# A column mean over 8192 rows: six row groups loaded in pairs instead of one by one, and no early load of group 60

## The chip, the cores and the metric

The kernel runs on one core of one Trainium2 chip. The metric is the device time of one execution in microseconds, as a median over runs. The engines are named as the profile names them: PE is TensorE (matrix multiplication), DVE is VectorE, ACT is ScalarE, POOL is GpSimd and SP is SyncE, which here issues nearly all DMA transfers.

## The reference

The kernel must compute the mean of each column of a float32 matrix of 8192 x 8192, 268 MB:

```
x = np.random.randn(8192, 8192).astype(np.float32)
np.mean(x, axis=0)
```

Every input element is read once and added once; the output is 8192 numbers. No part of the input is used twice.

## The kernel before, in words

The rows are cut into 64 groups of 128 (group g is the rows 128 g to 128 g + 127), and a group has one row on each of the 128 partitions, 8192 columns, 4096 KB. The columns are counted in sixteen blocks of 512. On chip there are six row buffers of that size: slots 0 to 3 receive loads, `both` (slot 4) holds the sum of a pair, and `acc` (slot 5) is the accumulator.

All loads are issued by SyncE in the order of the program, by the helper `load` (L75); a load waits, where its buffer was used before, for the add that read the buffer last. Two groups can come as one load (`load_rows`, L89): partition p then gets two neighbouring rows, 64 KB in one piece. Which row of a group of rows lands on which partition does not matter, since everything is summed in the end.

- L111 to L116: half a megabyte of group 60 (blocks 14 and 15) goes ahead into a buffer of its own, `early`; then the groups 0 to 3 as one load and 4 and 5 as another, and five blocks of group 63 (9 to 13), also into `early`. VectorE makes three adds of them that leave the sum in `acc`.
- L119 to L133, the main loop: two groups per load, slots 0 and 1 or 2 and 3 in turn. VectorE adds the two rows into `both` and then `both` into `acc`. It runs from group 6 to group 55. At groups 24 and 32, GpSimd adds the pieces in `early` into `acc`, in two parts.
- L135 to L138: groups 56 to 59 come one by one, and each is added straight into `acc`, one add per group.
- L139 to L144: group 60 comes without its last two blocks and VectorE adds fourteen blocks; group 61 comes whole and VectorE adds only the blocks 7 to 15. Blocks 0 to 6 of group 61 are left to TensorE.
- L145 to L152: group 62 comes whole. GpSimd adds its blocks 14, 15 and 8 into `acc` ("the joins" below, L148). Group 63 comes in four pieces (blocks 4 to 7, 0 to 3, 14 and 15, 8); its blocks 9 to 13 were loaded early.

TensorE makes the sums over the partitions, with a 128 x 32 matrix of 1/8192 as the weights, and can add several sources into one result: the accumulator, what is left of groups 61 and 62, and the pieces of group 63. Four column strips of TensorE work side by side: block i goes to strip i modulo 4, and the blocks 8 to 15 are spread over the strips in quarters (`spread`). The list `sums` (L167 to L181) gives the order, and TensorE keeps it: a matmul that waits holds back all behind it. At the end ScalarE and VectorE copy the results out of PSUM, and five small stores write the output; the last one (L219) writes block 8, whose sum over the last piece of group 63 comes last.

The order within each engine is the program's. An add that needs both a landing and the add before it gets the two waits by way of a no-op on ScalarE or GpSimd (L97 to L104), for which VectorE then waits.

Of the kernel before, what the change touches and what calls it, by code (L numbers as in the profile page):

```python
# [9 lines left out]
def kernel(  # L10
# [2 lines left out]
    x: bass.AP,  # L13
    out: bass.AP,
):

    nc = tc.nc
    f32 = mybir.dt.float32
    M, N = x.shape  # L40
    P = nc.NUM_PARTITIONS
    F = 512
    W = F // 4
    G = M // P
# [3 lines left out]
    sb = ctx.enter_context(tc.tile_pool(name="sb", bufs=1))  # L48
    psp = ctx.enter_context(tc.tile_pool(name="psum", bufs=1, space=bass.MemoryType.PSUM))

    bufs = sb.tile([P, U, N], f32, name="bufs")
    both = bufs[:, U - 2, :]
    acc = bufs[:, U - 1, :]
    ones = sb.tile([P, 32], f32, name="ones")
    early = sb.tile([P, 7 * F], f32, name="early")
    tail = sb.tile([P, W], f32, name="tail")
    warm = sb.tile([P, 32], f32, name="warm")
    nc.gpsimd.memset(ones[:], 1.0 / M)  # L58
# [16 lines left out]
    def load(dst, src):  # L75
        ins = tc.keep_in_program_order(nc.sync.dma_start(out=dst, in_=src)).ins  # L76
        k = len(loads)
        over = loads[k - 8:k - 6] if k >= 8 and k % 2 == 0 else []
        tc.declare_no_dep(ins, group="loads", keep=over, reason="the reader of the buffer waited")
        for o in over:  # L80
            tc.add_manual_dep(ins, o.name, sync, reason="covers the next load too")
        tc.add_to_no_dep_group("loads", ins)
        loads.append(ins)
        return ins

    def rows(g, n=1):
        return x[g * P:(g + n) * P, :]

    def load_rows(g, u, n):  # L89
        return load(bufs[:, u:u + n, :], rows(g, n).rearrange("(p j) c -> p j c", j=n))  # L90
# [3 lines left out]
    def add(dst, a, b, dmas):  # L94

        ins = nc.vector.tensor_add(out=dst, in0=a, in1=b).ins  # L96
        if dmas and adds:  # L97
            waiter = nc.scalar if len(adds) % 8 > 1 else nc.gpsimd
            nop = joins[waiter] = tc.keep_in_program_order(waiter.nop()).ins  # L99
            for o in dmas + adds[-1:]:  # L100
                tc.add_manual_dep(nop, o.name, sync, reason="the no-op waits")
            for group in ("loads", "adds"):
                tc.declare_no_dep(ins, group=group, reason="the no-op waited")
            tc.add_manual_dep(ins, nop.name, sync, reason="waits for both at once")  # L104
        elif adds:
            tc.declare_no_dep(ins, group="loads", reason="the add ahead waited")
        tc.declare_no_dep(ins, group="early", reason="the no-op waited, or the add behind it")
        tc.add_to_no_dep_group("adds", ins)
        adds.append(ins)

    load(early[:, 5 * F:], rows(G - 4)[:, 14 * F:])  # L111
    first, second = load_rows(0, 0, 4), load_rows(4, 4, 2)
    load(early[:, :5 * F], rows(G - 1)[:, 9 * F:14 * F])
    add(bufs[:, 2:4, :], bufs[:, 2:4, :], bufs[:, 0:2, :], [first])
    add(bufs[:, 4:6, :], bufs[:, 4:6, :], bufs[:, 2:4, :], [second])
    add(acc, acc, both, [])  # L116
    tc.keep_in_program_order(nc.scalar.copy(out=warm[:], in_=ones[:]))  # L117
    ahead = []
    g = 6  # L119
    while g < G - 8:  # L120
        u = (g + 2) % 4
        dma = load_rows(g, u, 2)
        add(both, bufs[:, u, :], bufs[:, u + 1, :], [dma])
        add(acc, acc, both, ahead)
        ahead = []
        if g in (24, 32):
            lo, hi = (0, 4) if g == 24 else (4, 7)
            cols = slice((9 + lo) * F, (9 + hi) * F)
            ins = tc.keep_in_program_order(nc.gpsimd.tensor_add(  # L129
                out=acc[:, cols], in0=acc[:, cols], in1=early[:, lo * F:hi * F])).ins  # L130
            tc.add_to_no_dep_group("early", ins)
            ahead = [ins]
        g += 2  # L133

    while g < G - 4:  # L135
        row = bufs[:, (g + 2) % 4, :]
        add(acc, acc, row, [load(row, rows(g))])
        g += 1  # L138
    for lo, hi, loaded in [(0, 14, 14), (7, 16, 16)]:  # L139
        row = bufs[:, (g + 2) % 4, :]  # L140
        dma = load(row[:, :loaded * F], rows(g)[:, :loaded * F])
        cols = slice(lo * F, hi * F)
        add(acc[:, cols], acc[:, cols], row[:, cols], [dma])
        g += 1  # L144
    r61, r62, r63 = [bufs[:, (g + 1 + j) % 4, :] for j in range(3)]  # L145
    load(r62, rows(g))
    for cols in [slice(14 * F, 16 * F), slice(8 * F, 9 * F)]:
        joined = tc.keep_in_program_order(nc.gpsimd.tensor_add(  # L148
# [7 lines left out]
    def blocks(row, lo, hi):  # L156
        for i in range(lo, hi):
            sums.append((banks[i // 4], i % 4, 0, row[:, i * F:(i + 1) * F]))
# [5 lines left out]
                at = lo * F + q * n + c  # L164
                sums.append((dst, q, c, row[:, at:at + min(F, n - c)]))

    blocks(acc, 2, 5)  # L167
    blocks(acc, 0, 2)
    blocks(r61, 0, 7)
    blocks(acc, 5, 8)  # L170
    blocks(r62, 0, 8)
    spread(wide, acc, 9, 14, slice(1))
    blocks(r63, 4, 8)
# [83 lines left out]
```

## Time and profile before

| what | us |
|---|---|
| median of three runs (628.39 to 628.57) | 628.53 |
| span of the profiled execution, first to last instruction | 626.4 |
| difference of the two | 2.1 |
| VectorE busy | 529.3 |
| TensorE busy | 13.3 |
| GpSimd busy | 12.0 |
| ScalarE busy | 3.7 |

The profile is of one execution, and its own time is given as its span; what lies around it is taken from the difference in the table. The page has a line of busy slices for each engine: the span is cut into 40, and a digit is the busy share in tenths. A group's line names source line, engine, operation, output and inputs with their sizes, and the count, then total busy time and the mean duration of one in ns, then the idle time ahead and what ended it. In the timeline a line has start, duration, engine, line and operation, the count of merged instructions, and in brackets the idle time before and its releaser. A releaser such as "ACTq L99" is the no-op of the helper, which in turn had waited for a landing. In the chain of waits a line has start, duration and what the time went to.

### The profile page before, as it was taken

The page shows a single profiled execution, that of the slowest core. Times are in us where ns is not written, and L with a number is a line of the kernel's source. Part 1 is how long each engine was busy: PE and PEld are TensorE (multiplying, and loading weights), DVE is VectorE, ACT ScalarE, POOL GpSimd, SP SyncE. Part 2 cuts the span into 40 slices and gives each one's busy share as a digit, 9 for nine tenths or more (in the row PEclk, how much of TensorE's full clock was granted, in tenths as well). Part 3 has the DMA queues.
Part 4 walks back from the last instruction along what each step waited for, and adds up shares of the span by engine and source line. Part 5 has one row for each costly group of instructions (what it writes and reads, how often), then busy time and mean ns, then how long its engine had stood idle before and what let it go on. Part 6 is the DMA issues. An engine that isn't in the chain of part 4 may idle for free.

```text
span 626.4 us, 484 instructions
## 1 busy us (share of the span) xinstructions
PE 13.3 (2%) x126; PEld 4.0 (1%) x126; DVE 529.3 (85%) x60; ACT 3.7 (1%) x6; POOL 12.0 (2%) x10
## 2 busy tenths in 40 slices
PE   0000000000000000000000000000000000000008
PEld 0000000000000000000000000000000000000002
DVE  0028999998888998889998899888898888999992
ACT  0000000000000000000000000000000000000001
POOL 0000000000000000020000200000000000000002
PEclk9999999999999999999999999999999999999999
DMA  8999999999999999999999999999999999999997
GB/s 372 465 402 428 459 410 460 402 469 402 469 402 469 402 469 402 469 402 469 402 465 406 439 431 427 444 410 460 402 469 402 469 402 469 402 435 435 419 435 305
DMA packets 5930, 268.50 MB, mean 429 GB/s; under 512 B 660, under 2 KB 668, under 8 KB 1064
## 3 DMA queue, kind: packets, MB, share of 16 engines
q1 hardware_dynamic: 5912, 268.46, 99.3%
q8 instruction: 1, 0.02, 0.0%
q10 hardware_dynamic: 16, 0.01, 0.0%
q14 instruction: 1, 0.01, 0.0%
HBM read 268.44 MB, written 0.03 MB: 429 GB/s over the span
## 4 chain that ended last, share of the span: by engine, by line
DMA 59%; DVE 30%; another core or an unknown queue 10%; issue 0%; SPq 0%; ACTq 0%; PE 0%; POOL 0%; POOLq 0%
DMA bufs<-in_x_dram 59%; DVE bufs L96 30%; SPq L76 0%; ACTq L99 0%; PE last L183 0%; DVE tail L214 0%; POOL ready L61 0%; POOL ones L58 0%; POOLq L99 0%; POOLq L241 0%
## 5 line engine op out<-in xcount | busy, mean ns | idle before, releaser
L96 DVE TENSOR_TENSOR bufs<-bufs 128x8192 f32<-128x8192 f32 (+3 forms) x59 | 529.0, 8966 | 85.9 <-DMA bufs<-in_x_dram 43.0
L183 PE MATMUL bank<-bufs,ones 128*32 128x512 f32 x62 | 10.0, 716 | 610.3 <-DVE bufs L96 610.0
L129 POOL TENSOR_TENSOR bufs<-bufs,early 128x2048 f32<-128x2048 f32 (+1 forms) x2 | 7.9, 3954 | 348.5 <-DVE bufs L96 348.5
L148 POOL TENSOR_TENSOR bufs<-bufs 128x1024 f32<-128x1024 f32 (+1 forms) x2 | 3.6, 1824 | 258.9 <-DMA bufs<-in_x_dram 258.9
L214 DVE COPY tail<-last 128x128 f32<-128x128 f32 x1 | 0.3, 291 | 8.8 <-PE last L183 8.8
L183 PEld LDWEIGHTS bank<-bufs,ones 128*32 128x32 f32 x62 | 2.2, 121 | 616.4 <-issue 614.5
L198 ACT COPY bufs<-bank 128x512 f32<-128x512 f32 x2 | 1.2, 586 | 617.9 <-PE bank L183 617.9
L183 PE MATMUL wide<-bufs,ones 128*32 128x512 f32 (+1 forms) x32 | 2.5, 432 | 0.0
L117 ACT ACT_TABLE_LOAD x1 | 1.3, 1283 | 0.7 <-PEq L241 0.7
L183 PE MATMUL two<-bufs,ones 128*32 128x256 f32 x16 | 1.2, 380 | 0.0
L183 PEld LDWEIGHTS wide<-bufs,ones 128*32 128x32 f32 x32 | 1.0, 110 | 1.8 <-issue 1.8
L183 PE MATMUL last<-bufs,ones 128*32 128x128 f32 x16 | 0.8, 279 | 0.1
L198 ACT COPY bufs<-wide 128x640 f32<-128x640 f32 x1 | 0.7, 692 | 1.1 <-PE wide L183 1.1
L183 PEld LDWEIGHTS last<-bufs,ones 128*32 128x32 f32 x16 | 0.4, 109 | 1.2 <-issue 0.6
L183 PEld LDWEIGHTS two<-bufs,ones 128*32 128x32 f32 x16 | 0.4, 109 | 0.1
L198 ACT COPY bufs<-two 128x256 f32<-128x256 f32 x1 | 0.4, 372 | 0.1
L117 ACT COPY warm<-ones 128x32 f32<-128x32 f32 x1 | 0.2, 217 | 0.0
L61 POOL TENSOR_TENSOR ready<-ones 128x1 f32<-128x1 f32 x1 | 0.2, 193 | 0.1
L58 POOL MEMSET ones<- 128x32 f32 x1 | 0.1, 125 | 0.3 <-POOLq L241 0.3
L241 POOL MEMSET const-float32-0.0<- 128x1 f32 x1 | 0.1, 98 | 0.2 <-issue 0.2
L241 POOL MEMSET const-bfloat16-1.0<- 128x1 bf16 x1 | 0.1, 102 | 0.0
L241 POOL MEMSET const-uint8-127<- 128x1 uint8 x1 | 0.1, 102 | 0.0
(1 smaller groups left out, 0.1 us busy)
## 6 DMA issues: line engine op xcount, KB each, us to landing
bufs<-in_x_dram SPq DMA_DIRECT2D x6, 4096.0 KB, 20.4
bufs<-in_x_dram SPq DMA_DIRECT2D x1, 3584.0 KB
bufs<-in_x_dram SPq DMA_DIRECT2D x2, 1024.0 KB, 18.7
early<-in_x_dram SPq DMA_DIRECT2D x1, 1280.0 KB
early<-in_x_dram SPq DMA_DIRECT2D x1, 512.0 KB
bufs<-in_x_dram SPq DMA_DIRECT2D x1, 512.0 KB, 19.4
bufs<-in_x_dram SPq DMA_DIRECT2D x27, 29.9
bufs<-in_x_dram SPq DMA_DIRECT2D x1, 256.0 KB, 19.7
```

What stands on the lines that cost most here:

```text
L58: nc.gpsimd.memset(ones[:], 1.0 / M)
L61: nc.gpsimd.tensor_add(out=ready[:], in0=ones[:, 0:1], in1=ones[:, 1:2]))
L96: ins = nc.vector.tensor_add(out=dst, in0=a, in1=b).ins
L117: tc.keep_in_program_order(nc.scalar.copy(out=warm[:], in_=ones[:]))
L129: ins = tc.keep_in_program_order(nc.gpsimd.tensor_add(out=acc[:, cols], in0=acc[:, cols], in1=early[:, lo * F:hi * F])).ins
L148: joined = tc.keep_in_program_order(nc.gpsimd.tensor_add(out=acc[:, cols], in0=acc[:, cols], in1=r62[:, cols])).ins
L183: summed = tc.keep_in_program_order(nc.tensor.matmul(out=dst[32 * q:32 * q + 32, c:c + cols.shape[1]], lhsT=ones[:], rhs=cols, start=all(( ...
L198: return tc.keep_in_program_order(nc.scalar.copy(out=dst, in_=src)).ins
L214: ended = nc.vector.tensor_copy(out=tail[:], in_=last[:]).ins
L241: nc = _bacc.Bacc("TRN2", target_bir_lowering=False, num_devices=1)
```

## The change

Groups 56 to 61 come as three loads of two groups, where they were six loads of one. Groups 56 to 59 are now part of the main loop: both rows into `both`, then into `acc`. Group 60 comes whole beside group 61, so nothing of it is loaded early, and `early` holds only the five blocks of group 63; GpSimd adds them in parts of three and two blocks (they were four and three, with the two blocks of group 60 at the end). VectorE adds all sixteen blocks of group 60 and then the blocks 7 to 15 of group 61; both adds follow the same landing. TensorE's list begins with the seven blocks of group 61, then the blocks 0 to 7 of the accumulator, which before stood around them. What follows in the list is the same.

```diff
-    early = sb.tile([P, 7 * F], f32, name="early")
+    early = sb.tile([P, 5 * F], f32, name="early")
...
-    load(early[:, 5 * F:], rows(G - 4)[:, 14 * F:])
     first, second = load_rows(0, 0, 4), load_rows(4, 4, 2)
-    load(early[:, :5 * F], rows(G - 1)[:, 9 * F:14 * F])
+    load(early[:], rows(G - 1)[:, 9 * F:14 * F])
...
-    while g < G - 8:
+    while g < G - 4:
...
-            lo, hi = (0, 4) if g == 24 else (4, 7)
+            lo, hi = (0, 3) if g == 24 else (3, 5)
...
-    while g < G - 4:
-        row = bufs[:, (g + 2) % 4, :]
-        add(acc, acc, row, [load(row, rows(g))])
-        g += 1
-    for lo, hi, loaded in [(0, 14, 14), (7, 16, 16)]:
-        row = bufs[:, (g + 2) % 4, :]
-        dma = load(row[:, :loaded * F], rows(g)[:, :loaded * F])
-        cols = slice(lo * F, hi * F)
-        add(acc[:, cols], acc[:, cols], row[:, cols], [dma])
-        g += 1
-    r61, r62, r63 = [bufs[:, (g + 1 + j) % 4, :] for j in range(3)]
+    u = (g + 2) % 4
+    dma = load_rows(g, u, 2)
+    add(acc, acc, bufs[:, u, :], [dma])
+    r61 = bufs[:, u + 1, :]
+    add(acc[:, 7 * F:], acc[:, 7 * F:], r61[:, 7 * F:], [])
+    g += 2
+    r62, r63 = [bufs[:, (g + 2 + j) % 4, :] for j in range(2)]
     load(r62, rows(g))
...
-    blocks(acc, 2, 5)
-    blocks(acc, 0, 2)
     blocks(r61, 0, 7)
-    blocks(acc, 5, 8)
+    blocks(acc, 0, 8)
     blocks(r62, 0, 8)
```

## The prediction

> **What bounds the kernel now.** I read the page's busy slices first, then the timeline of the last 120 us, then the chain of waits, and last the windows around the final matmuls.
>
> The page: the DMA engines are full from end to end, VectorE is busy 85%, TensorE only in the last slice.
>
> ```profile
> span 626.4 us, 484 instructions
> ...
> PE   0000000000000000000000000000000000000008
> ...
> DVE  0028999998888998889998899888898888999992
> ...
> DMA  8999999999999999999999999999999999999997
> ```
>
> VectorE's timeline: a pair of groups costs 17.42 us and starts every 19.35 us (510.81, 530.16, 549.50), each time after 1.93 us of idling for the landing. So the stream of loads sets the pace. From 549.50, where the single groups begin to arrive, VectorE runs without a gap, 65.39 us and eight adds.
>
> ```profile
> 510.81 17.42 DVE L96 TENSOR_TENSOR bufs<-bufs 128x8192 f32<-128x8192 f32 x2 [1.94 <-ACTq L99]
> 530.16 17.42 DVE L96 TENSOR_TENSOR bufs<-bufs 128x8192 f32<-128x8192 f32 x2 [1.93 <-POOLq L99]
> 549.50 65.39 DVE L96 TENSOR_TENSOR bufs<-bufs 128x8192 f32<-128x8192 f32 x8 [1.93 <-ACTq L99]
> ```
>
> The same timeline at the end: group 62 lands at 616.28 (TensorE's wait is ended by DMA), after VectorE has finished at 614.9. From 616.28 TensorE works through the remaining sums almost without a gap, and meets the last landing at 623.2.
>
> ```profile
> 616.28 1.92 PE L183 MATMUL bank<-bufs,ones 128*32 128x512 f32 x16 [0.28 <-DMA bufs<-in_x_dram]
> 616.49 3.61 POOL L148 TENSOR_TENSOR bufs<-bufs 128x1024 f32<-128x1024 f32 x2 [258.93 <-DMA bufs<-in_x_dram]
> ...
> 623.23 0.43 PE L183 MATMUL last<-bufs,ones 128*32 128x128 f32 x8
> 623.73 0.29 DVE L214 COPY tail<-last 128x128 f32<-128x128 f32 x1 [8.83 <-PE last L183]
> 624.04 0.50 SPq L201 DMA_DIRECT2D out_dram<-tail  x1
> ```
>
> The chain of waits names the last landing as what the end follows:
>
> ```profile
> 603.45 19.74 DMA bufs<-in_x_dram
> 623.19 0.04 issue
> 623.23 0.47 PE last L183 x8
> ```
>
> So two things end together: the stream (623.19) and TensorE's own work on groups 62 and 63, which had only some 0.26 us of slack (the 256-column sums of group 63 start their second pass at 622.76 and need 0.21 us, so the last sums could have started near 622.97). Anything that delays TensorE's start on group 62 shows at the end almost whole.
>
> **The change, part by part.**
>
> *The loads.* Bytes are the same, only order and size change. Without the early half megabyte of group 60 the first load starts earlier. Its share of the stream: 19.35 us carry 8192 KB, so 512 KB is 1.2 us. Bounds: 0, if the start-up of the first load hides it, and 1.65 us, from the first packet of the early load (1.78 us) to the first large packet (3.4 us) in the DMA records. I take 1.2, the price at the stream's own rate. All later pairs land 1.2 earlier: pair 54 at 549.44 - 1.2 = 548.24, and then pairs 56, 58 and 60 every 19.35: 567.6, 586.9, **606.3**. In before group 61 alone landed at about 616.23 - 9.7 = 606.5, so the stream is worth 0.2 us. Three issues fewer on SyncE (0.33 us each) lie beside transfers that are already queued.
>
> *Issue times.* Group 62's load now waits for the first add of pair 58, which ends at 586.9 + 0.06 + 8.70 = 595.7; the stream is busy with pair 60 until 606.3, a cover of 10.6 us. The four pieces of group 63 go behind it without a VectorE wait, near 597 instead of 602.1. Cost 0.
>
> *GpSimd's early adds* shrink by a block each (from 4.49 and 3.42 us; the 1024-column row is 2.37). VectorE's add beside them is longer (11.21 and 10.12 instead of 8.70 in the chain), but it waits 1.93 us per pair for the stream anyway, and the next load is queued ten microseconds ahead: 0. Without that cover it would be at most 2.5 us once.
>
> *VectorE's last adds*, the term that matters. Single groups let VectorE take 56 to 60 one by one, and only nine blocks of 61 (4.96 us) were left behind group 60. As pairs, 56/57 and 58/59 are worked in their 19.35 us again (17.42 us, idle 1.9 before the next). Then pair 60 lands at 606.3, with all its work still to do:
>
> ```profile
> L96 DVE TENSOR_TENSOR bufs<-bufs 128x8192 f32<-128x8192 f32 x55 | 482.0, 8763 | 40.5 <-ACTq L99 30.6 <-POOLq L99 8.2
> ...
> L96 DVE TENSOR_TENSOR bufs<-bufs 128x4608 f32<-128x4608 f32 x1 | 5.0, 4957 | 0.1
> ```
>
> 606.3 + 0.06 (landing to add, as 549.44 to 549.50) + 8.70 (group 60, undisturbed) + 0.02 + 4.96 (nine blocks) = **620.04**, against 614.9 before: 5.1 us later, and 3.8 us past the time at which group 62 was taken up. The no-op for group 60 stands in GpSimd's queue, ahead of the two joins, which need the same add: nothing else waits there.
>
> *TensorE.* Seven blocks of group 61 run from 606.3, blocks 0 to 6 of the accumulator from 615.1, and block 7 needs the last add, so it starts at 620.09. Behind it, in order, stand all sums over group 62. Block 7 writes the fourth column strip, which block 3 of group 62 needs too; a block's two passes take 0.87 us (eight blocks on four strips from 616.28 to 618.02). So that strip takes up group 62 at 620.09 + 0.87 = 620.96 where it was 616.28: +4.68. The wait for the last landing (0.26) is gone, as group 63 lands by about 623. Sum at the end: **+4.4 us**. Block 7's round is the unknown: 0 if the strips fill the gap, 0.87 if its strip stays last. I take 0.87, since that strip has the same number of pieces as the others.
>
> *GpSimd's joins* (2.37 + 1.28 us) move from 616.5 to about 620.2 and end at 623.9. The 256-column sums need the first at 620.96 + 4.75 = 625.7, the 128-column ones at about 627: 3 us of slack, cost 0. *Stores and copies* keep their distances behind TensorE, so the 2.7 us from the last matmul to the end of the span remain.
>
> *TensorE's rate.* This is the second unknown. The same sixteen matmul instructions took twice as long right after idling as later:
>
> ```profile
> 609.98:613.41 3.43, 3.43 (x16) 0.77 (x17) 0.00 (x0) 1.00 1.07 459
> ...
> 616.28:618.02 1.74, 1.74 (x16) 0.41 (x16) 0.00 (x0) 1.00 1.03 428
> ```
>
> (Windows of the bank sums: stretch, its length, TensorE busy, weight loads, ScalarE, granted clock, DMA share, GB/s.) The granted-clock column says 1.00 in both, so the slow stretch is read from the durations. In before those slow 3.43 us lay ahead of group 62's landing, and the 0.4 us pause before it did not bring them back. Now there are three bursts: 606.3 to about 609.8, 615.1 to 616.9 or 618.5, and the last from 620.1, with pauses of 5.3 and of 1.6 to 3.2 us. If the last burst runs full speed, the extra cost is 0. If it starts slow, 3.43 us of it do half their work: +1.7; the worst I give it is a second stretch of the same, +3.4. I take 0, since the second burst comes between and, if it runs slow, is as long as the stretch after which the rate doubled in before.
>
> [...]
>
> **Sum.** +4.68 - 0.26 = +4.4 on a span of 626.4: 630.8. The median shown (628.53) is 2.1 us above that span; I keep this distance. **632.9 us**, 0.7% slower. A measurement of this kernel tells about 0.2% (1.3 us) from no change.
>
> **The rivals.**
>
> *TensorE starts its last burst slow.* For it: the 3.43 us row, and two new pauses. Against: a pause of 0.4 us did nothing, and the second burst warms it. It gives 632.9 + 1.7 = 634.6, between 633.4 and 636.3.
>
> *The adds stay beside the transfers* (the other side). If the stream delivered pair 60 early enough that VectorE ended before 616.28 - 0.87 + 0.26 = 615.7, the last landing would set the end again, at about 628.3. That needs pair 60 at 602.0 instead of 606.3: three pairs in 53.8 us, 17.9 each. Against it: 23 pairs from 104.37 to 549.44 took 19.35 each, and the stream's 432 GB/s is the same in that stretch and in the stretch of the single groups.
>
> *The early load is worth more and block 7's round is hidden*: -0.45 and -0.87 give 631.6, about 631.0 to 632.1.
>
> **How the numbers follow.** Forecast 0.66 (its own range 632.1 to 633.4), slow burst 0.28, smaller delay 0.04, adds hidden 0.02. The range 632.1 to 635.0 leaves out the last two (0.06) and the upper part of the slow burst (about 0.1). Slower holds all but the hidden case: 0.98; that case is split into 0.01 and 0.01. The early load's lower bound of 0 would give 634.1 and lies inside.
>
> **What would show it.** In the changed kernel: VectorE's adds in pairs of 17.42 us every 19.35 us up to pair 58, then one run of 8.70 + 4.96 us from about 606.3 to 620.0; TensorE idle until then, and its wait before the last burst ended by VectorE instead of DMA; GpSimd's joins released by VectorE; no wait for a landing in the chain's last 14 us. I am wrong if pair 60 lands elsewhere than 605.8 to 607.5, if the last burst is not about 8 us long (longer: slow clock), or if TensorE takes up group 62 before VectorE is done.

## The result and the profile after

The changed kernel takes 633.84 us in the median of four runs (633.27 to 634.82), against 628.55 (628.39 to 628.81): a ratio of 1.0088, 95% interval 1.0074 to 1.0101. That is 5.3 us slower; 632.9 was forecast.

The page of the changed kernel (span, busy slices; one line each for TensorE, VectorE, granted clock and DMA):

```profile
span 633.0 us, 472 instructions
...
PE   0000000000000000000000000000000000000037
...
DVE  0038999989888898889898888988888988889882
...
PEclk9999999999999999999999999999999999999987
DMA  9999999999999999999999999999999999999993
```

The DMA line was full to its last slice before (7 tenths there); now the last slice holds 3 tenths while TensorE works alone. And the clock line, all nines before, ends in 8 and 7. Next the timeline of VectorE and GpSimd in the changed kernel:

```profile
568.28 17.42 DVE L74 TENSOR_TENSOR bufs<-bufs 128x8192 f32<-128x8192 f32 x2 [1.94 <-ACTq L77]
587.63 17.42 DVE L74 TENSOR_TENSOR bufs<-bufs 128x8192 f32<-128x8192 f32 x2 [1.93 <-ACTq L77]
606.99 13.68 DVE L74 TENSOR_TENSOR bufs<-bufs 128x8192 f32<-128x8192 f32 x2 [1.94 <-POOLq L77]
...
620.75 3.59 POOL L121 TENSOR_TENSOR bufs<-bufs 128x1024 f32<-128x1024 f32 x2 [264.85 <-DVE bufs L74]
```

Pairs 56 and 58 keep the 19.35 us rhythm with the idle 1.9 us, and the last pair's 13.68 us start at 606.99 and end at 620.67. GpSimd's joins are released by VectorE, where a landing released them before. So are TensorE's second and last bursts (a burst is a run of matmuls between two pauses); before, a landing ended the wait ahead of group 62:

```profile
615.74 3.64 PE L154 MATMUL bank<-bufs,ones 128*32 128x512 f32 x14 [5.36 <-DVE bufs L74]
620.73 3.73 PE L154 MATMUL bank<-bufs,ones 128*32 128x512 f32 x17 [1.35 <-DVE bufs L74]
```

The chain of waits has no landing after 606.93:

```profile
577.00 29.93 DMA bufs<-in_x_dram
606.93 0.04 POOLq L77
606.97 0.02 issue
606.99 8.70 DVE bufs L74
615.70 0.02 issue
615.72 4.97 DVE bufs L74
620.69 0.04 issue
620.73 3.73 PE bank L154 x17
```

Last, windows of TensorE over its bursts, in the changed kernel (stretch, its length, TensorE busy and instructions, granted clock, DMA share, GB/s):

```profile
607.07:610.38 3.31, 3.31 (x14) 1.00 1.01 436
615.74:619.38 3.64, 3.63 (x14) 0.50 1.01 421
620.73:623.58 2.85, 2.85 (x16) 0.50 0.55 216
623.58:630.07 6.49, 6.48 (x88) 1.00 0.02 4
```

The clock records of this profile begin at 609.92, and time ahead of them counts as 1.00; the 14 instructions in 3.31 us show that the first burst ran at the slow rate too. The last burst runs at half the clock until 623.58. From block 7 (620.73) to VectorE's copy (630.09) it takes 9.36 us.

### The profile page after: what moved, and what is told of

Read it like the earlier page. It is cut to its first block, busy times and chain, and to the rows that moved or that the text cites. A ratio compares the mean times of both kernels' runs of the same rounds, so it can differ in the third digit from the quotient of the medians.

```text
span 633.0 us, 472 instructions
## 1 busy us (share of the span) xinstructions
PE 16.3 (3%) x126; PEld 5.7 (1%) x126; DVE 528.2 (83%) x60; ACT 3.7 (1%) x6; POOL 9.9 (2%) x10
## 4 chain that ended last, share of the span: by engine, by line
DMA 61%; DVE 27%; another core or an unknown queue 10%; PE 1%; issue 0%; POOL 0%; POOLq 0%; ACTq 0%
DMA bufs<-in_x_dram 61%; DVE bufs L74 27%; PE bank L154 1%; PE wide L154 0%; PE two L154 0%; PE last L154 0%; POOLq L77 0%; ACTq L77 0%; DVE tail L185 0%; POOL ready L39 0%; POOL ones L36 0%; POOLq L212 0%
## 5 line engine op out<-in xcount | busy, mean ns | idle before, releaser
L74 DVE TENSOR_TENSOR bufs<-bufs 128x8192 f32<-128x8192 f32 (+2 forms) x59 | 527.9, 8948 | 92.8 <-DMA bufs<-in_x_dram 42.4
L154 PE MATMUL bank<-bufs,ones 128*32 128x512 f32 x62 | 14.2, 885 | 613.8 <-DMA bufs<-in_x_dram 607.1
L106 POOL TENSOR_TENSOR bufs<-bufs,early 128x1536 f32<-128x1536 f32 (+1 forms) x2 | 5.8, 2878 | 349.0 <-DVE bufs L74 349.0
L154 PE MATMUL wide<-bufs,ones 128*32 128x512 f32 (+1 forms) x32 | 4.0, 432 | 0.0
```

Of the source, the lines that this page charges most:

```text
L106: ins = tc.keep_in_program_order(nc.gpsimd.tensor_add(out=acc[:, cols], in0=acc[:, cols], in1=early[:, lo * F:hi * F])).ins
L154: summed = tc.keep_in_program_order(nc.tensor.matmul(out=dst[32 * q:32 * q + 32, c:c + cols.shape[1]], lhsT=ones[:], rhs=cols, start=all(( ...
```

## The experiments

**Which of the loads carries the loss.** One kernel pairs only the last two groups, the other only the four ahead of them.

```diff
 # against the changed kernel: pair 60/61 alone
-    while g < G - 4:
+    while g < G - 8:
...
+    while g < G - 4:
+        row = bufs[:, (g + 2) % 4, :]
+        add(acc, acc, row, [load(row, rows(g))])
+        g += 1
     u = (g + 2) % 4
     dma = load_rows(g, u, 2)
```

> The changed kernel with groups 56 to 59 as four single loads again; only groups 60 and 61 come as a pair. Theory (the two adds behind the last pair's landing set VectorE's end): VectorE is done with group 59 near 602 and waits for the pair, which lands near 607.0 as in the changed kernel, so its last add ends at 620.7 and the time is that of the changed kernel, 633.3 at full TensorE speed and up to 634.8 with a slow last burst. Rival (the loss is spread over all three pairs, because VectorE works two rows late in each): two thirds of the loss come back, about 630.3.

Measured: 633.57 us (633.07 to 635.37), 1.0089 of the kernel before (1.0075 to 1.0103): the whole loss. VectorE's timeline of this run:

```profile
548.85 52.60 DVE L74 TENSOR_TENSOR bufs<-bufs 128x8192 f32<-128x8192 f32 x6 [1.93 <-ACTq L77]
607.08 13.69 DVE L74 TENSOR_TENSOR bufs<-bufs 128x8192 f32<-128x8192 f32 x2 [5.63 <-POOLq L77]
```

VectorE had caught up at 601.45 and then waited 5.63 us for the pair, and the 13.69 us behind the landing end where they end in the changed kernel. The rival, that the loss is spread over all three pairs, would have shown about 630.3; it falls. One of the four runs, 635.37, lies above the 634.8 that the expectation allowed; its mean granted clock is 0.992, that of the other three 1.000.

```diff
 # against the kernel before: pairs 56/57 and 58/59 alone
-    while g < G - 8:
+    while g < G - 4:
...
-    while g < G - 4:
-        row = bufs[:, (g + 2) % 4, :]
-        add(acc, acc, row, [load(row, rows(g))])
-        g += 1
```

> The kernel before with groups 56 to 59 as two pairs in the main loop; groups 60 and 61 stay single and the early load stays. Theory: VectorE is busy with pair 58 until 588.1 + 0.06 + 17.42 = 605.6, then 7.63 for fourteen blocks of group 60 and 4.96 for nine of group 61: 618.3, which is 2.1 past the landing of group 62. With block 7's round of 0.87 and the slack of 0.26 the time is 628.55 + 2.7 = 631.3, up to 1.7 more if TensorE's last burst is slow. Rival (the loss is in the last pair alone): 628.5, as before.

Measured: 631.80 us (631.35 to 632.13), ratio 1.0055 (1.0041 to 1.0069). VectorE's last four adds:

```profile
588.18 30.21 DVE L96 TENSOR_TENSOR bufs<-bufs 128x8192 f32<-128x8192 f32 x4 [1.94 <-ACTq L99]
```

They end at 618.39 where 618.3 was worked out; from there to the copy of the last sum at 627.04 VectorE waits 8.66 us, where the run with the last pair alone waits 8.03 us, its last burst at a granted clock of 1.00. That these 0.6 us, which make up the 0.5 above 631.3, are a slow start of the last burst is an estimate: no view of this run shows the clock there. So each pairing alone delays VectorE's end, the first by 3.5 us and the last by 5.9, and the two don't add: the later landing hides the earlier one. Not all of the 5.9 is the pairing itself: two blocks of group 60 are no longer loaded early, so its add takes 8.70 us where it took 7.63 before. Those 1.07 us come from the early load that is gone; no run pairs groups 60 and 61 and keeps that load.

**What the early half megabyte is worth.**

```diff
 # against the kernel before
-    load(early[:, 5 * F:], rows(G - 4)[:, 14 * F:])
...
-    for lo, hi, loaded in [(0, 14, 14), (7, 16, 16)]:
+    for lo, hi, loaded in [(0, 16, 16), (7, 16, 16)]:
```

(`early` and GpSimd's two parts as in the changed kernel.)

> The kernel before with group 60 loaded whole, no early half megabyte, and VectorE adding all sixteen blocks of group 60; loads stay single. Theory from the trace of the changed kernel (the first landing came only 0.59 us earlier, though 512 KB are 1.2 us of the stream): the stream ends 0.6 later, group 62 lands near 616.85, VectorE is done by 615.4, and the time is 629.1. Rival (the early load costs what its bytes cost): the stream ends as before, 628.55, or a little later by VectorE's two extra blocks, if these count (1.06 us: 629.6).

Measured: 628.61 us (628.17 to 628.99, eleven runs) against 628.28 (628.07 to 628.75, fifteen); ratio 1.0005, interval 0.9996 to 1.0014. The difference is within what can be told, so neither side is shown by the time. Its profile, taken in the slowest of the eleven runs, leans to the theory: the first add starts at 42.11, 0.88 earlier than the 42.99 of before and not 1.2, and group 62 is taken up at 616.74 instead of 616.28.

**Whether TensorE's order is part of it.**

```diff
 # against the changed kernel
-    blocks(acc, 0, 8)
+    blocks(acc, 0, 7)
     blocks(r62, 0, 8)
+    blocks(acc, 7, 8)
```

> The changed kernel with one change in TensorE's list: the eight blocks of group 62 go ahead of block 7 of the accumulator. VectorE and the loads are untouched, so its last add still ends at 620.7. Theory (all sums over group 62 stand in order behind block 7): 1.74 us of TensorE's work moves ahead of 620.7 and the time falls to about 631.5 at full TensorE speed, to 633 if the burst is slow for part. Rival (VectorE's end alone sets the time, TensorE's order does not matter): 633.3 to 634.8, as the changed kernel.

Measured: 631.26 us (631.04 to 631.39), ratio 1.0046 (1.0030 to 1.0061). VectorE's last two adds are the same 13.68 us, from 606.48. TensorE's timeline in this run:

```profile
615.23 6.08 PE L155 MATMUL bank<-bufs,ones 128*32 128x512 f32 x32 [5.09 <-DVE bufs L74]
621.13 1.03 PE L155 MATMUL wide<-bufs,ones 128*32 128x512 f32 x8
```

Group 62's sums now run in the burst that starts at 615.23, and no pause is left ahead of block 7. The rival is out: VectorE's end sets the time only together with what stands behind it in TensorE's list.

**TensorE's clock.** First the changed kernel once more, then with idle work (matmuls whose result nobody reads) in its pauses.

> The changed kernel itself, without an edit, for the spread of its times beside the next run. [...]

Measured: 634.87 us (634.73 to 635.23, four runs); with the first four runs, eight: 633.27, 633.30, 634.37, 634.73, 634.78, 634.82, 634.95 and 635.23. These four alone spread 0.5 us; with the first four the eight spread 2.0 and lie in two heaps. The mean granted clock on record parts them: 0.995 and 1.000 in the two runs at 633.3, 0.992 in each of the six others. Windows of this run:

```profile
615.37:619.01 3.64, 3.63 (x14) 0.50 0.98 410
620.36:624.60 4.24, 4.24 (x20) 0.50 0.48 188
624.60:630.39 5.79, 5.78 (x82) 1.00 0.01 4
```

Here the half clock lasts to 624.60, and the last burst (620.36 to the copy at 630.42) is 10.06 us.

```diff
 # against the changed kernel; spare is a PSUM tile that nobody reads
+    def filler(n):
+        for i in range(n):
+            sums.append((spare, i % 4, 0, early[:, :F]))
+
     blocks(r61, 0, 7)
-    blocks(acc, 0, 8)
+    filler(20)
+    blocks(acc, 0, 7)
+    filler(8)
+    blocks(acc, 7, 8)
```

> The changed kernel with idle work added to TensorE, whose result nobody reads: twenty 512-column matmuls between group 61's blocks and the accumulator's block 0, and eight ahead of the accumulator's block 7. They lie in TensorE's pauses (5.3 us and 1.4 to 3.2 us) and end before 620.7. Theory (part of the loss is TensorE's last burst at half speed after the pauses): every run is at full speed from 620.7 on, the last burst takes 8.0 us, the times are 633.2 within 0.4, and the upper runs at 634 to 635 are gone. Rival (the spread comes from landings or from elsewhere, not from TensorE's clock): times from 633.3 to 634.8 as without them, or later, if the added matmuls get in the way.

Measured: 632.89 us (632.75 to 633.20, five runs), beside 634.87 on the same chip. Windows of this run:

```profile
612.40:619.06 6.66, 6.66 (x60) 1.00 0.97 410
620.17:622.00 1.83, 1.82 (x18) 1.00 0.98 388
622.00:628.12 6.12, 6.11 (x86) 1.00 0.04 14
```

The clock is full from 612.40 on, the burst from 620.17 to the copy at 628.14 takes 7.97 us, and the upper runs are gone. More work on TensorE made the kernel 2.0 us faster. The rival (spread from landings) falls: pair 60's add started at 606.43 here and at 606.62 in the run without the idle work, so landings give 0.2 us of the difference of the two profiles, and the last burst 2.1.

**Less behind the last add.**

```diff
 # against the changed kernel
-    add(acc[:, 7 * F:], acc[:, 7 * F:], r61[:, 7 * F:], [])
+    add(acc[:, 8 * F:], acc[:, 8 * F:], r61[:, 8 * F:], [])
...
-    blocks(r61, 0, 7)
+    blocks(r61, 0, 8)
```

> The changed kernel with eight blocks of group 61 left to TensorE instead of seven, so VectorE's last add is eight blocks (4.43 instead of 4.96 us) and block 7 of the accumulator no longer waits for it. Theory (what costs is the work that stands in TensorE's order behind the last add): the last add ends at 620.2, only sums over blocks 8 to 15 wait for it, group 62's 1.74 us and block 7's 0.87 us move ahead; 630.5 at full speed, to 631.5 where the earlier burst is slow. Rival (the end follows VectorE's last add at a fixed distance): 633.3 - 0.5 = 632.8.

Measured: 630.90 us (630.21 to 631.67), ratio 1.0042 (1.0028 to 1.0056), with the median within the theory's values and 1.9 below the rival's 632.8. The two faster runs (630.21 and 630.60) have a mean granted clock of 1.000, the two slower ones (631.20 and 631.67) 0.995. VectorE's line of this run:

```profile
606.42 13.15 DVE L74 TENSOR_TENSOR bufs<-bufs 128x8192 f32<-128x8192 f32 x2 [1.95 <-POOLq L77]
```

VectorE's adds behind the landing became 0.5 us shorter (13.15 instead of 13.68); the time fell by 2.4 even against the lowest run of the changed kernel.

```diff
 # against the kernel just above; spare and filler as in the run with idle work
     blocks(r61, 0, 8)
+    filler(20)
     blocks(acc, 0, 8)
     blocks(r62, 0, 8)
-    spread(wide, acc, 9, 14, slice(1))
-    blocks(r63, 4, 8)
     spread(wide, r62, 9, 14, slice(1))
+    blocks(r63, 4, 8)
+    spread(wide, acc, 9, 14, slice(1))
     for row in (acc, r62):
         spread(wide, row, 9, 14, slice(1, 2))
-    spread(two, acc, 14, 16)
     blocks(r63, 0, 4)
-    spread(last, acc, 8, 9)
+    spread(two, acc, 14, 16)
     spread(two, r63, 14, 16)
+    spread(last, acc, 8, 9)
     spread(last, r63, 8, 9)
```

> The run before this one, with the twenty added matmuls of idle work after group 61's blocks, and TensorE's list in the order in which data comes: group 62 and blocks 4 to 7 of group 63 ahead of all that needs VectorE's last add. Theory: TensorE has only 2.3 us of work left that needs the last add (620.2); the end is then set by GpSimd's joins, which start at 620.2 and end near 623.9, and by the last landing near 623.5; 628.9, within 0.1% of the kernel before. Rival (group 60's and 61's adds behind one landing cost 4 us whatever TensorE does): above 630.5.

Measured: 629.35 us (629.06 to 629.74, ten runs) against 628.35; ratio 1.0016 (1.0007 to 1.0025). VectorE still ends its last adds 13.15 us behind the landing of pair 60, but TensorE's wait is for a load again:

```profile
622.27 1.06 PE L161 MATMUL bank<-bufs,ones 128*32 128x512 f32 x8 [0.41 <-DMA bufs<-in_x_dram]
```

So all but 1.0 us of the loss goes without touching the loads: by order, by one block and by the clock. The rival's 630.5 is excluded. The 628.9 was not quite reached. In this profile the piece of group 63 that TensorE waits for landed at 622.23, against 621.04 in the run above, and the last piece at 624.11, against 622.94 there and 623.19 before (39 GB/s from 622.23 to 624.11 here, 3 GB/s from 622.33 to 622.94 there); whether these late landings are in all ten runs, and so are the reason, is not shown. No version beat the kernel before.

## Why the prediction was right, and where it was off

- **The bound moves from the stream to VectorE's two adds behind the last landing: right, and shown.** The adds took 8.70 and 4.97 us, as in the sum; the run that pairs 60 and 61 alone has the whole loss.
- **TensorE takes up group 62 a block-7 round later: right.** With the clock full, the last burst is 7.97 us (filler run; the run with the last pair alone has 620.82 to 628.79, also 7.97) where the sum's terms, block 7's round (0.87), the work from 616.28 to 622.97 (6.69) and the last sums (0.47), make 8.03. Moving group 62 ahead of block 7 took 2.0 us off the least of the changed kernel's times (633.27).
- **The early load: the size was off.** 1.2 us were taken at the stream's rate; the first landing came 0.6 earlier in the profile after, and the second load, which landed at 62.35 before, came 0.8 earlier on average over the eight profiles without the early load (0.6 to 1.1). In the profile after, pair 60 landed at 606.93 instead of 606.3, which is 0.6 of the miss there; in five of the other runs it landed between 606.36 and 606.56. The first landing alone doesn't set this: in the run with the last pair alone it came 0.9 earlier, and the pair still landed at 607.01.
- **TensorE's rate: the step that failed.** The prediction put: "If the last burst runs full speed, the extra cost is 0", and "I take 0", with a chance of 0.66. Only two of eight runs of the changed kernel fit that (633.27 and 633.30); the others are 1.1 to 2.0 us above them. The profiles measure the term at 1.4 us (9.36 against 7.97) and 2.1 us (10.06), a burst longer than 8 us as the prediction's own sign of a slow clock had it. What failed is the reason, "the second burst warms it": that burst (3.64 us) ran at half clock and left the clock there. Its other reason, a pause of 0.4 us that did nothing, misreads the row, which shows 0.28 us. The rival of the slow burst was the common case in the changed kernel, within its price (1.7, between 0.5 and 3.4); it adds to the forecast's mechanism and doesn't replace it. So the median, 633.84, lies above the forecast's own 632.1 to 633.4 and inside the rival's 633.4 to 636.3: the stated range held because it took in the lower part of the rival's, not because this term was right. The filler run, 632.89, shows the forecast's 632.9 with this term at 0. A little luck is in that agreement: from the copy to the end of the span it takes 3.0 us instead of 2.7, and the time lies 1.8 above the span instead of 2.1, which cancel.
- The rest held: joins released by VectorE with no wait behind them, no cost from issue times (the change saves four load issues, not the three that the prediction counted), and no landing in the chain's last 14 us.

For the profiled execution the sum closes: the copy of the last sum starts at 630.09 instead of 623.73, 6.36 later; 4.4 by the prediction's sum, 0.6 by the later landing and 1.4 by the half clock make 6.4.

In both profiles of the changed kernel the slow last burst follows the new pause: TensorE did nothing from 610.38 to 615.74 in the profile after and from 610.34 to 615.37 in the other, and the second burst stands at a granted clock of 0.50 in both. In the profile after, the clock is 1.00 from 609.92 to 613.34, with 0.46 us of work in that stretch, and 0.50 from 613.34 to 623.58. The pause alone does not decide it: in the run with the last pair alone it is 5.08 us, the second burst takes the same 3.64 us, and the last burst takes 7.97 us at 1.00. What sets the moment of the fall is not shown. The rival's 634.6 is among the six upper runs (634.37 to 635.23).

## What to carry to other kernels

At the end of a stream of loads, count what has to be done after each landing: joining the last two loads puts the work of the first of them behind the landing, even where the bytes arrive no later (VectorE's end came 5.9 us later in the run with the last pair alone). What is issued in order behind the last result belongs to that cost, and reordering alone won back at least 2.0 us here, with the adds as long as they were. Where TensorE waits between short bursts, as here, price the half rate for the last burst as a case of its own: six of eight runs of the changed kernel (634.37 to 635.23) and one of four with the last pair alone (635.37) have a mean granted clock of 0.992, and with the pauses filled all five runs (632.75 to 633.20) have 0.999 or 1.000.

## What the runs showed of the hardware that was not expected

- A burst of 3.64 us ran at half clock and left it there. The granted clock in the profile after is 1.00 from 609.92 to 613.34 (3.42 us), 0.50 in the next 10.24 us, and 1.00 again from 623.58. Windows of TensorE, as long as the first of these stretches:

```profile
606.51:609.92 3.41, 2.85 (x14) 1.00 1.05 452
609.92:613.34 3.42, 0.46 (x3) 1.00 1.07 460
616.75:620.16 3.41, 2.62 (x14) 0.50 1.00 416
620.16:623.58 3.42, 2.85 (x16) 0.50 0.63 247
```

  The second burst, from 615.74 to 619.38, has 2.62 us of its work between 616.75 and 620.16, and the clock is still at 0.50 behind it. The last burst starts at 620.73 at 0.50 and is at 1.00 after 2.85 us. How much work brings the clock back, no run shows. The time until then differs between executions: 2.85 us of the last burst in this profile, 4.24 us (620.36 to 624.60) in the other one of the changed kernel, with pair 60's add starting at 606.99 and 606.62. A prediction has then to price both cases.
- A DMA record of 16 KB on the instruction queue, about 1.1 us long, is among the records from 619 to 625 in the run by arrival (1.1% of the sixteen engines' time there); in the profile before one is among those from 622.4 to 623 (11.2%), in the profile after among those from 624 to 630 (1.2%). Whether it bears on the late landing of the last pieces of group 63 in the run by arrival is not shown, and no run tried it.
